# Modulation-weight loads asked for one step later: the ring of buffers keeps one load less ahead

## Chip, cores and metric

The kernel runs on one core of a Trainium2 chip. The metric is the device time of one execution in microseconds (us). Five engines work side by side, each on its own list of instructions in program order: TensorE (PE in the profile, its weight loads PEld), VectorE (DVE), ScalarE (ACT), GpSimd (POOL) and SyncE (SP). In this kernel SyncE computes nothing; its list is a queue of transfers that it issues one after the other, each as soon as what that transfer has to wait for is done.

## What is computed

One step of a two-layer transformer that serves 256 prompt tokens and 1024 latent tokens, width 1024, all in float32. Each layer has a token mixer and a SwiGLU channel mixer. What bears on the change is the modulation: both sub-layers of a layer are scaled, shifted and gated by vectors that come from a conditioning vector, one for latent tokens and one for the prompt.

```
mod_p = silu(c_ctx) @ w_mod[l] + b_mod[l]      # (6*1024,), w_mod[l] is (1024, 6144)
mod_s = silu(c)     @ w_mod[l] + b_mod[l]
sh1, sc1, g1, sh2, sc2, g2 = split(mod, 6)     # for each of the two
x = x + g1 * mixer(rms_norm(x) * (1 + sc1) + sh1)
x = x + g2 * swiglu(rms_norm(x) * (1 + sc2) + sh2)
```

The matrices w_mod hold 2 x 1024 x 6144 numbers, some 50 MB, and are read once.

## The kernel before

The stages follow each other: input projection of layer 0, its attention, its output projection (`out_proj`), its channel mixer (`ffn`), then the same four for layer 1. Weights of the dense products come through `Weights`: a 512 KB piece is loaded into `wraw` or `wrawx` (L251), and split into a high and a low part `whl` by ScalarE (L280) and VectorE (L282) four pieces ahead of use. When a piece has been split, its buffer is given back and the next 512 KB load goes into SP's queue.

The modulation vectors of later sub-layers are made in the background of these stages by the class `Mod`, on VectorE. A job is 512 columns of `w_mod` for one layer; it has 8 tiles of 128 x 512 (256 KB). One call of `step` takes one tile: two VectorE instructions (L386 or L388) multiply it by the two conditioning columns and add it to two accumulators `nacc`. After the eighth tile two calls do nothing, then two calls sum the accumulators over the partitions (four transposes on TensorE each, L400, and a VectorE reduction, L401), and a last call adds the bias (`mod_done`, L324). So a job takes 13 calls, 8 of which use a tile.

The tiles sit in a ring of `bufs` buffers. The constructor asks for the first `bufs` loads; then each step that has used a tile asks for a further one (L318 through `load`). Program order alone decides where that transfer stands in SP's queue. There are four rings:

- input projection of layer 0: 4 jobs, `bufs` 4, tile `wmod`; up to two steps for each dense product
- output projection of layer 0: 2 jobs, `bufs` 3, tile `wmod`; two steps after a dense product
- channel mixer of layer 0: 12 jobs, 96 tiles, `bufs` 2, the two halves of one tile `st`
- channel mixer of layer 1: 2 jobs, 16 tiles, `bufs` 2, the same

In `ffn` a hidden slice i (22 of them) goes through `front`, `prompt_gate` and `back`. From i = 2 on, each slice calls `mstep`, which is one `step`, six times, here in the order of the program, with the transfers that are put into SP's queue between the calls:

```
front(i):  product Q11, mstep, product Q21 -> c (L925)
prompt_gate(i):                W.done       -> weight load (L251)
back(i):   product T2 (L1004), mstep
           product T1,         W.done       -> weight load, mstep
           product T3 (L1017), mstep
           product Q22 (L1027) -> spill of H (L900), W.done -> weight load, mstep
           prompt product -> spill (L945), product T4 -> spill (L900),
                               W.done       -> weight load, mstep
```

The last `mstep` of a slice and the first of the next have only the product Q11 between them, which ScalarE reads out; so VectorE does their four instructions in a row. The weight load ahead of that pair waits for the L282 that VectorE does just before the pair.

After the slices come six rounds `down(q)` that multiply the stored hidden values `hd` by the down weights (matmuls L1063 to L1065, each result added into `x` by VectorE at L1067). Round q loads its slabs `A<-hd` by `load_h` (L905, three transfers of 1 to 2 MB), asked for two rounds ahead, and `load_x` brings back `x<-xr` (L911, 24 transfers). In the rounds one `mstep` follows each output row block. PSUM results of the dense stages use a ring of 8 banks (`psd`).

Of the kernel before, what the change touches and what calls it, by code (L numbers as in the profile page):

```python
# [123 lines left out]
def hybrid_step(ctx: ExitStack, tc: tile.TileContext, I: dict, O: list):  # L124
# [67 lines left out]
    class Background:  # L192
# [12 lines left out]
        def step(self, n=1, now=1 << 30):  # L205
            for _ in range(n):
                if not self.q or self.q[0][1] > now or self.q.pop(0)[2]():
                    return
# [112 lines left out]
    def mod_done(l, j, v):  # L321

        o = modv[:, l, 4 * j:4 * j + 4, :]
        dve.tensor_tensor(o, v, bmod[:, l, 4 * j:4 * j + 4, None].to_broadcast([128, 4, 2]), op=OP.add)  # L324
        six, half = j // 2, j % 2
        if six in (1, 4):
            k = six // 4
            g = norms[:, 2 * l + k, 4 * half:4 * half + 4, None].to_broadcast([128, 4, 2])
            dve.scalar_tensor_tensor(moda[:, l, k, 4 * half:4 * half + 4, :], o, 1.0, g, op0=OP.add, op1=OP.mult)
# [27 lines left out]
    class Mod:  # L357
# [14 lines left out]
        def step(self):  # L372
            if self.pending:
                f = self.pending.pop(0)
                if f:
                    f()
                return True
            if self.pos >= len(self.tiles):
                return False
            l, j, k = self.tiles[self.pos]  # L380
            t = self.loaded.pop(self.pos)[:, 0]
            if k == 0:
                self.acc = [(self.sums or npool).tile([128, 512], F32, name="nacc", bufs=2) for _ in range(2)]
            for c, a in enumerate(self.acc):
                if k == 0:
                    dve.tensor_scalar(a, t, cond_raw[:, k, c:c + 1], 0.0, op0=OP.mult, op1=OP.add)  # L386
                else:
                    dve.scalar_tensor_tensor(a, t, cond_raw[:, k, c:c + 1], a, op0=OP.mult, op1=OP.add)  # L388
            self.pos += 1
            self.load(self.pos + self.bufs)  # L390
            if k == 7:
                acc, v = self.acc, npool.tile([128, 32], F32, name="mv", bufs=2)[:, 0:8].rearrange("p (b x) -> p b x", x=2)
                self.pending = [None, None, lambda: self.sum(acc[0], v, 0), lambda: self.sum(acc[1], v, 1),
                                lambda: mod_done(l, j, v)]
            return True
# [1326 lines left out]
```

## Time and profile before

| | us |
|---|---|
| median of 3 runs | 3082.54 |
| lowest, highest | 3079.99, 3093.14 |
| the profiled execution, its own time | 3094.04 |
| its span, first to last instruction | 3092.3 |
| mean granted clock of TensorE in it | 0.975 |

The profiled execution is one run; 1.7 us of its time lie outside the span. It is 11.5 us above the median of the three unprofiled runs. Times within the trace are counted from the start of the span.

### The profile page before, as it was taken

What the parts mean: (1) busy time and instruction counts of PE and PEld (TensorE: products, weight loads), DVE (VectorE), ACT (ScalarE), POOL (GpSimd) and SP (SyncE); (2) the same over time, 40 slices, a digit from 0 to 9 for tenths busy, and PEclk for the clock granted to TensorE, in tenths of its full rate; (3) what the DMA queues carried; (4) which work ended last, traced back from release to release, by engine and by line L of the source; (5) the groups of instructions that cost most, each with busy time, mean ns of one, the idle gap of its engine ahead of it and who ended that gap; (6) DMA issues with size and microseconds to landing.
All of it is one profiled execution on the core that took longest, in us unless ns stands there. A gap on an engine that the chain in (4) does not pass through costs nothing.

```text
span 3092.3 us, 46174 instructions
## 1 busy us (share of the span) xinstructions
PE 2937.8 (95%) x18074; PEld 2489.7 (81%) x18074; DVE 1875.6 (61%) x3035; ACT 1089.3 (35%) x2084; POOL 822.8 (27%) x692
## 2 busy tenths in 40 slices
PE   6999999988999999899999999999789999999998
PEld 4878777867888887788878777878678888888887
DVE  5654665577777776544455688862767555554334
ACT  4233773343333332000332577761433333330002
POOL 0241542232333332000222344431323333320002
PEclk9999999989999999999999999999899999999999
DMA  6467644213434436543133410123033223255421
GB/s 248 146 194 228 154 128 154 89 49 129 136 127 130 133 126 237 203 172 138 68 122 141 154 59 31 36 83 99 24 130 116 92 93 101 102 180 204 177 102 69
DMA packets 184330, 394.55 MB, mean 128 GB/s; under 512 B 32176, under 2 KB 69424, under 8 KB 177840
## 3 DMA queue, kind: packets, MB, share of 16 engines
q1 hardware_dynamic: 180656, 385.34, 36.7%
q0 software_dynamic: 3456, 6.26, 0.8%
q8 instruction: 143, 2.34, 0.3%
q14 instruction: 75, 0.61, 0.1%
HBM read 274.32 MB, written 118.23 MB: 127 GB/s over the span
## 4 chain that ended last, share of the span: by engine, by line
PE 68%; DVE 11%; ACT 5%; issue 3%; POOL 3%; DMA 2%; SPq 0%; DVEq 0%; ACTq 0%; POOLq 0%
PE psd L1063 6%; PE psd L1065 6%; PE psd L1064 6%; PE psd L307 6%; PE psd L309 6%; PE psd L308 6%; PE psd L884 6%; PE psd L885 6%; PE psd L886 6%; PE ps_t L684 5%; PE ps_o L700 5%; PE ps_s L632 4%; DVE nacc L388 2%; ACT whl L280 2%; DVE whl L282 2%
## 5 line engine op out<-in xcount | busy, mean ns | idle before, releaser
L308 PE MATMUL psd<-A,whl 128*128 128x256 f32 (+1 forms) x1760 | 585.9, 333 | 16.0 <-DVE A L490 15.0
L307 PE MATMUL psd<-A,whl 128*128 128x256 f32 (+1 forms) x1760 | 588.9, 335 | 7.3 <-ACT A L454 2.7
L309 PE MATMUL psd<-A,whl 128*128 128x256 f32 (+1 forms) x1760 | 583.1, 331 | 2.0 <-DVE whl L282 2.0
L280 ACT ACTIVATE whl<-wraw 128x1024 fp32r<-128x1024 f32 x178 | 187.1, 1055 | 649.7 <-PE psd L1065 461.2
L1063 PE MATMUL psd<-A,whl 128*128 128x512 f32 (+1 forms) x1056 | 378.1, 358 | 16.3 <-DVE x L1067 10.3
L308 PEld LDWEIGHTS psd<-A,whl 128*128 128x128 f32 x1760 | 341.6, 194 | 52.5 <-DVE A L490 17.5
L1064 PE MATMUL psd<-A,whl 128*128 128x512 f32 (+1 forms) x1056 | 376.1, 356 | 0.0
L1065 PE MATMUL psd<-A,whl 128*128 128x512 f32 (+1 forms) x1056 | 376.0, 356 | 0.0
L307 PEld LDWEIGHTS psd<-A,whl 128*128 128x128 f32 x1760 | 342.2, 194 | 41.3 <-ACT A L454 3.2
L309 PEld LDWEIGHTS psd<-A,whl 128*128 128x128 f32 x1760 | 346.0, 197 | 31.7 <-DVE whl L282 3.3
L1067 DVE SCALAR_TENSOR_TENSOR x<-psd,modv,x 128x512 f32<-128x512 f32 (+1 forms) x288 | 186.9, 660 | 283.1 <-PE psd L1065 278.8
L282 DVE TENSOR_TENSOR whl<-wraw,whl 128x1024 fp32r<-128x1024 f32 x174 | 238.7, 1374 | 145.4 <-ACT whl L280 143.3
L884 PE MATMUL psd<-A,whl 128*128 128x512 f32 x704 | 277.4, 394 | 0.0
L885 PE MATMUL psd<-A,whl 128*128 128x512 f32 x704 | 275.4, 391 | 0.0
L886 PE MATMUL psd<-A,whl 128*128 128x512 f32 x704 | 275.4, 391 | 0.0
L674 POOL TENSOR_SCALAR sP<-sP,sm 128x896 f32<-128x896 f32 (+2 forms) x206 | 179.4, 875 | 245.8 <-DVE sm L667 120.0
L1063 PEld LDWEIGHTS psd<-A,whl 128*128 128x128 f32 x1056 | 201.1, 190 | 45.5 <-DVE x L1067 11.1
L1065 PEld LDWEIGHTS psd<-A,whl 128*128 128x128 f32 x1056 | 202.1, 191 | 28.0
L1064 PEld LDWEIGHTS psd<-A,whl 128*128 128x128 f32 x1056 | 201.1, 190 | 27.6
L684 PE MATMUL ps_t<-ident,sP 128*128 128x128 f32 x1408 | 206.6, 285 | 7.3 <-POOL sP L674 2.6
L426 POOL TENSOR_TENSOR nacc<-nacc,ec 128x512 f32<-128x512 f32 (+1 forms) x32 | 34.7, 1084 | 623.2 <-ACT ec L425 621.8
L684 PEld LDWEIGHTS ps_t<-ident,sP 128*128 128x128 f32 x1408 | 152.8, 143 | 57.3 <-issue 24.5
(224 smaller groups left out, 5246.6 us busy)
## 6 DMA issues: line engine op xcount, KB each, us to landing
hd<-x SPq DMA_DIRECT2D x84, 512.0 KB, 3.1
A<-hd SPq DMA_DIRECT2D x20, 2048.0 KB, 12.3
wraw<-in_w_gu_dram SPq DMA_DIRECT2D x60, 512.0 KB, 3.6
st<-in_w_mod_dram SPq DMA_DIRECT2D x112, 256.0 KB, 2.8
wraw<-in_w_down_dram SPq DMA_DIRECT2D x44, 512.0 KB, 3.7
wrawx<-in_w_gu_dram SPq DMA_DIRECT2D x28, 512.0 KB, 3.7
A<-hd SPq DMA_DIRECT2D x14, 1024.0 KB, 14.8
wmod<-in_w_mod_dram SPq DMA_DIRECT2D x48, 256.0 KB, 3.0
```

The costliest lines, as they stand in the source:

```text
L280: act.activation(h[:, 0], src, AF.Copy)
L282: eng.tensor_tensor(h[:, 1], src, h[:, 0].bitcast(F32), op=OP.subtract)
L307: pe.matmul(ps[:, :n], wh, A[ti].part(0, k), start=(k == 0), stop=False)
L308: pe.matmul(ps[:, :n], wh, A[ti].part(1, k), start=False, stop=False)
L309: pe.matmul(ps[:, :n], wl, A[ti].part(0, k), start=False, stop=(k == 7))
L684: pe.transpose(pt[:, 128 * (i - lo):128 * (i - lo) + 128], P[u][:, 128 * j:128 * j + 128], ident)
L884: pe.matmul(pt, wh, t(0, c), start=(c == 0), stop=False)
L885: pe.matmul(pt, wh, t(1, c), start=False, stop=False)
L886: pe.matmul(pt, wl, t(0, c), start=False, stop=(c == 3))
L1063: pe.matmul(pt[:, :n], wh, t[:, 0, k], start=(k == 0), stop=False)
L1064: pe.matmul(pt[:, :n], wh, t[:, 1, k], start=False, stop=False)
L1065: pe.matmul(pt[:, :n], wl, t[:, 0, k], start=False, stop=(k == nk - 1))
```

## The change

`step` asks for loads up to `pos + bufs - 1` in place of `pos + bufs`. The constructor still asks for `bufs` loads. So the first step asks for none, and from the second step on each step asks for the load that the step before it asked for until now: each later load stands in SP's queue where the next one stood. The buffer it goes into is the same and the step that must have used that buffer is the same; what is new is that all transfers that the program puts into SP's queue between two steps now stand ahead of it. The number of loads, their size and all arithmetic stay.

```diff
             self.pos += 1
-            self.load(self.pos + self.bufs)
+            self.load(self.pos + self.bufs - 1)
             if k == 7:
```

## Rows read from the trace of the kernel before

**Rows 1.** Windows: stretch, us, busy of PE, PEld, DVE, ACT, POOL, clock, DMA, GB/s.

```profile
711.00:1208.00 497.00, 482.71 (x2594) 418.71 (x2593) 383.85 (x463) 157.59 (x234) 169.97 (x112) 0.99 0.40 131
1208.00:1265.00 57.00, 41.36 (x177) 34.07 (x175) 33.12 (x51) 5.24 (x8) 2.75 (x2) 0.85 0.85 308
1265.00:1440.00 175.00, 175.00 (x924) 151.00 (x923) 88.77 (x128) 13.62 (x13) 0.00 (x0) 1.00 0.44 160
```

**Rows 2.** Waits of VectorE, 711 to 1208: us in total, times, longest us.

```profile
DVE whl L282 <- ACT whl L280: 49.8, 46, 1.9
...
DVE ea L1027 <- POOL ea L1018: 9.0, 7, 1.5
```

**Rows 3.** Waits of TensorE, 711 to 1208.

```profile
PE psd L400 <- DVE nacc L388: 14.3, 3, 8.1
```

**Rows 4.** Timeline of SP: start us, duration, what; two stretches of the slices.

```profile
734.68 0.52 SPq L900 DMA_DIRECT2D hd<-x  x1
736.91 0.33 SPq L251 DMA_DIRECT2D wraw<-in_w_gu_dram  x1
738.24 7.31 SPq L318 DMA_DIRECT2D st<-in_w_mod_dram  x3
...
940.48 0.33 SPq L251 DMA_DIRECT2D wrawx<-in_w_gu_dram  x1
```

**Rows 5.** Timeline of VectorE: pairs of steps, first, fifth and ninth; in brackets idle time.

```profile
736.81 2.73 DVE L388 SCALAR_TENSOR_TENSOR nacc<-st,cond_raw,nacc 128x512 f32<-128x512 f32 x4
...
940.37 3.76 DVE L388 SCALAR_TENSOR_TENSOR nacc<-st,cond_raw,nacc 128x512 f32<-128x512 f32 x4
...
1124.29 2.73 DVE L388 SCALAR_TENSOR_TENSOR nacc<-st,cond_raw,nacc 128x512 f32<-128x512 f32 x4
```

**Rows 6.** Timeline of SP, start of the third ring.

```profile
705.83 0.33 SPq L251 DMA_DIRECT2D wrawx<-in_w_gu_dram  x1
706.22 5.54 SPq L318 DMA_DIRECT2D st<-in_w_mod_dram  x3
```

**Rows 7.** Timeline of VectorE, first step of the third ring.

```profile
710.52 0.88 DVE L386 TENSOR_SCALAR nacc<-st,cond_raw 128x512 f32<-128x512 f32 x2 [4.71 <-DMA st<-in_w_mod_dram]
```

**Rows 8.** Page, part 6: DMA issues, KB each, median us to landing.

```profile
st<-in_w_mod_dram SPq DMA_DIRECT2D x112, 256.0 KB, 2.8
```

**Rows 9.** Timeline of TensorE, single rows where it waited.

```profile
554.66 0.63 PE L400 MATMUL psd<-ident,nacc 128*128 128x128 f32 x4 [3.24 <-DVE nacc L388]
...
1080.62 0.66 PE L400 MATMUL psd<-ident,nacc 128*128 128x128 f32 x4 [3.41 <-DVE nacc L388]
...
1219.60 0.55 PE L1063 MATMUL psd<-A,whl 128*128 128x256 f32 x1 [5.36 <-DMA A<-hd]
...
1253.71 0.79 PE L1063 MATMUL psd<-A,whl 128*128 128x512 f32 x1 [6.48 <-DVE x L1067]
...
2319.48 1.11 PE L400 MATMUL psd<-ident,nacc 128*128 128x128 f32 x4 [9.93 <-DVE nacc L388]
```

**Rows 10.** Timeline of SP, end of the slices and first down round.

```profile
1200.95 1.31 SPq L905 DMA_DIRECT2D A<-hd  x2
...
1229.46 0.84 SPq L318 DMA_DIRECT2D st<-in_w_mod_dram  x1
...
1231.42 2.02 SPq L905 DMA_DIRECT2D A<-hd  x3
```

**Rows 11.** Timeline of VectorE, first down round.

```profile
1222.55 1.41 DVE L388 SCALAR_TENSOR_TENSOR nacc<-st,cond_raw,nacc 128x512 f32<-128x512 f32 x2
...
1236.65 1.41 DVE L388 SCALAR_TENSOR_TENSOR nacc<-st,cond_raw,nacc 128x512 f32<-128x512 f32 x2 [7.80 <-DMA st<-in_w_mod_dram]
...
1251.85 1.41 DVE L388 SCALAR_TENSOR_TENSOR nacc<-st,cond_raw,nacc 128x512 f32<-128x512 f32 x2 [9.04 <-DMA st<-in_w_mod_dram]
1253.18 1.80 DVE L1067 SCALAR_TENSOR_TENSOR x<-psd,modv,x 128x256 f32<-128x256 f32 x3
```

**Rows 12.** Timeline of VectorE, last step of the first ring.

```profile
263.75 1.42 DVE L388 SCALAR_TENSOR_TENSOR nacc<-wmod,cond_raw,nacc 128x512 f32<-128x512 f32 x2 [3.62 <-DMA wmod<-in_w_mod_dram]
```

## Prediction

> **What bounds the kernel now.** I read the profile by stages, with the sums by window first. In most stretches TensorE is never idle, so only what makes it wait counts. Three stretches hold steps of the rings with two buffers: the slices of the first channel mixer, its first down round, and the later rounds [rows 1]. In the slices TensorE is busy 482.71 of 497 us and VectorE 383.85, which looks like room on VectorE. The waits say otherwise. VectorE's waits in this stretch come to seven groups, and none of them names TensorE; the largest are for ScalarE and GpSimd instructions that themselves had to wait for a VectorE result just before [rows 2]. So VectorE runs behind TensorE all through these 497 us, and its list, with the round trips in it, is a chain without slack. TensorE feels this chain at one place only: the transposes of a finished job wait for the accumulators, three times, 14.3 us in all [rows 3]. A microsecond that VectorE loses between two such ties is therefore not absorbed; it is handed to TensorE at the next tie.
>
> **What the change does.** It removes and adds no instruction. Load n keeps its buffer, so it still waits for step n - bufs. It only moves behind the transfers that stand between its old place in SP's queue and that of load n+1. Where no transfer stands between, nothing changes. Where some do, they wait for later VectorE work, so the load is issued when the last of them has been. Whether a step is late then depends on how soon it follows.
>
> In a slice, five of six places are harmless: the step that uses the load comes after another product result, some microseconds later. The sixth is the pair of steps in a row. The load for its second step now stands behind the two spills and the weight load that precede the pair. In the first pair, the steps start at 736.81 and their four instructions take 2.73, so the second begins at about 738.1 [rows 5]. The weight load was issued at 736.91, the spill at 734.68 [rows 4]. The moved load can go no earlier than right behind that weight load, some 0.4 us later.
>
> *How late it lands.* The nearest row of before is the start of the third ring: a spill, a 512 KB weight load at 705.83 and the modulation load at 706.22, 0.39 us behind it [rows 6]; the step that needs it starts at 710.52, 4.69 us after the weight load was issued [rows 7]. By that row the second step of the pair starts at 736.91 + 4.69 = 741.60, not 738.1: VectorE stands 3.5 us. The lower bound is a load that nothing in front delays, 2.8 us [rows 8]: 736.91 + 0.39 + 2.8 = 740.1, 2.0 us. As 512 KB are ahead of it in the same queue, I stay near the upper row: 3.3.
>
> The Trainium skill (DMA: Bandwidth & Descriptors, Anatomy of one DMA) fits a transfer issued from GpSimd as 2.0 us plus its bytes at 436 GB/s. As an estimate by that page these 256 KB would take 2.6 us and the stall would be 1.8; nine of them would be 16 us in place of the 28 that I use below, and the whole sum 22, a time of 3104. The rows show this load at 2.8 in the median and at over 4 behind a weight load, so the fit lacks what stands ahead.
>
> *How many.* Nine such pairs lie in the slices of the first channel mixer, from 736.81 to 1124.29; in two of them the first step itself takes about a microsecond longer (as in the fifth, 3.76 for the four) and uses up that much of the stall [rows 5]. 7 x 3.3 + 2.3 + 2.8 = 28.2 us on VectorE. In a tenth pair only the spills are ahead, and I count it as 0.
>
> *Where they come out.* Eight of the nine lie before 1080.62, where TensorE already waits 3.41 us for an accumulator, so it takes over the whole delay there: 24.9. The ninth lies behind it. At 1219.60 TensorE waits 5.36 us for a slab [rows 9], and that slab's load is at the end of a queue that only went on, at 1200.95, when VectorE had split a weight [rows 10]. There the remaining 3.3 come out. Sum: **+28**.
>
> **The first down round.** Here VectorE already waits for modulation loads, 7.80 and 9.04 us, while TensorE stands because its PSUM banks are full [rows 9, 11]. Each load takes the place of the next. So the step at 1222.55, which did not wait, gets the landing that now ends the wait at 1236.65, and the one that now runs at 1236.65 goes directly behind it; the one that lands at 1251.85 serves the step before the one it serves now. VectorE comes out one cycle late: a step of 1.41 and three results of 1.80 together, **+3.2**, and TensorE with it, since the banks of three results are released that much later. The bounds are 0, if TensorE regained it (it doesn't wait at all from 1265 to 1440 [rows 1], so there is nothing to regain), and 7 if the longer idling also costs clock: the granted clock in this stretch is 0.85 against 1.00 behind it [rows 1].
>
> **The later rounds.** Some loads there come behind three slab loads. How long that takes is seen at 1231.42 [rows 10]: the modulation load behind those three serves the step at 1251.85 [rows 11], 20 us later. A round has a step each 7 us, so two steps, behind the two such places with a job under way, will be up to 10 us late. I count this as nothing, and the cover is the ring of PSUM banks: 924 matmuls take 175 us [rows 1], 36 of them make a row of three results, 6.8 us, so TensorE can run eight results, 18 us, ahead. Without that cover it would be up to 20.
>
> **The second channel mixer** has two such pairs. The first stands directly ahead of the job end at 2319.48, where TensorE waits 9.93 us [rows 9]: **+3.3**. Behind the second no step is left after that job, and VectorE can catch up: 0.
>
> **The other rings.** In the output projection a load moves behind a weight load and makes one of the last steps about 0.8 us late; TensorE waits for that job's end at 554.66 [rows 9]: **+0.8**, bounds 0 and 1.5. In the input projection the next to last load moves behind the load of a K slab and lands with the last, which VectorE awaits at 263.75; one step of 1.42 us then comes later [rows 12]. Two calls without work and further products follow before the sums, which cover it: 0, bound 1.4.
>
> **Sum.** 28 + 3.2 + 3.3 + 0.8 = 35.3 us. The profiled execution took 3094.04, so its like would take 3129. Its distance to the median is not the change's, so the same sum on the median of 3082.54 gives **3118**.
>
> **Rivals.**
> - *Only the ties count.* If VectorE catches up between the ends of jobs, just the stalls right ahead of a tie come through: two in the first mixer, one in the second, with the down round and the output projection 3 x 3.3 + 3.2 + 0.8 = 14, so 3096. For it: TensorE passes most job ends without waiting (three in [rows 3]). Against it: VectorE never once waits for TensorE in the stretch [rows 2], so it has nothing to catch up with.
> - *Hidden anyway.* If the load, though later in the queue, landed before its step, or ran ahead of the weight load, the slices would not change; what is left is the down round, +3: 3086. It decides if the landing takes under 0.8 us from issue, and no row comes near [rows 8].
> - *Faster: the queue comes free.* With the load's wait gone from in front of the slab loads, slabs could come earlier, at best the whole wait of 5.36 at 1219.60 [rows 9]: 3077. Against it: what follows a moved load in the queue waits for VectorE instructions that come after the step anyway.
> - *Worse by the clock.* TensorE's new waits at the job ends bring stretches at the lower of its two clocks, as around 1208 to 1265; 0.15 of these 57 us once more [rows 1] is 8.6, so 3127.
>
> **How the numbers follow.** My forecast, VectorE's chain in full: 0.68. Only the ties: 0.14. Hidden anyway: 0.07. Faster queue: 0.02. Worse by the clock: 0.09. 0.5% of the median, about what a measurement of this kernel can tell from no change, is 15.4 us: 3067 to 3098. The forecast and the clock case lie above that; the ties case, at 3096, straddles the bound, a third of it above; the hidden and the faster queue lie within, but for a small part of the last. Slower 0.81, same 0.18, faster 0.01. The range leaves out the hidden and faster cases and reaches from the ties case, 3096, to the clock case with stalls of 3.5, 3130.
>
> **What would show it.** Right: in each of the nine pairs VectorE idles 2 to 3.5 us in the middle, released by a modulation load issued 0.4 us after a weight load; waits of L388 for `st`, which the slices do not have now, come to some 28 us; TensorE's waits at L400 grow by some 25 us; the step that was at 1222.55 waits over 10 us. Wrong: pairs without a gap (then the load is not late), or gaps that do not appear at L400 or in the span (then VectorE had slack after all).

## The result, and the profile after

| | before | after |
|---|---|---|
| median of four runs, us | 3084.85 | 3123.76 |
| lowest, highest, us | 3079.99, 3093.14 | 3120.55, 3125.97 |
| the profiled execution, us | 3094.04 | 3125.97 |
| mean granted clock of TensorE in it | 0.975 | 0.971 |

The ratio is 1.0123, with a 95% interval from 1.0098 to 1.0147: 38 us slower, between 30 and 45, in place of the 35.3 forecast; the 3123.76 lie within the range given. The profiled executions are 31.9 us apart; that of before lies above all four runs in the table (3093.14 at most), and that of after is the slowest of its four. Layer 0 ran 3.3 us faster in the trace of after, up to the first step of the third ring (707.18, against 710.52 in [rows 7]). So times of after compare with those of before when 3.33, the difference before rounding, is added; I do so below where I speak of a delay.

The windows of after, laid over the same three stretches as [rows 1]:

```profile
707.00:1234.00 527.00, 492.14 (x2612) 424.56 (x2611) 383.96 (x461) 157.42 (x233) 170.44 (x112) 0.97 0.36 124
1234.00:1296.00 62.00, 39.87 (x172) 32.91 (x171) 35.83 (x56) 6.32 (x8) 2.70 (x2) 0.78 0.75 280
1296.00:1468.00 172.00, 172.00 (x911) 148.50 (x910) 85.26 (x126) 12.74 (x12) 0.00 (x0) 1.00 0.43 163
```

VectorE's 384 us of work in the slices are the same; the stretch is 30 us longer. What fills them stands in VectorE's waits from 707 to 1236, the answer to [rows 2]:

```profile
DVE whl L282 <- ACT whl L280: 53.0, 47, 1.9
DVE nacc L388 <- DMA st<-in_w_mod_dram: 28.5, 10, 4.7
...
DVE ea L1027 <- POOL ea L1018: 9.0, 7, 1.5
```

The second row is new: ten waits, 28.5 us. TensorE is still in none of these rows. The first of the ten, as SP and then VectorE saw it:

```profile
731.36 0.52 SPq L900 DMA_DIRECT2D hd<-x  x1
733.59 0.33 SPq L251 DMA_DIRECT2D wraw<-in_w_gu_dram  x1
733.97 5.60 SPq L318 DMA_DIRECT2D st<-in_w_mod_dram  x3
```

```profile
733.48 1.40 DVE L388 SCALAR_TENSOR_TENSOR nacc<-st,cond_raw,nacc 128x512 f32<-128x512 f32 x2
737.80 1.42 DVE L388 SCALAR_TENSOR_TENSOR nacc<-st,cond_raw,nacc 128x512 f32<-128x512 f32 x2 [2.92 <-DMA st<-in_w_mod_dram]
```

What was one row of four instructions in [rows 5] is two rows with a hole of 2.92 us. The load goes out 0.38 us behind the weight load and its step starts 3.83 us after that. In the nine pairs of the slices the holes are 2.92, 3.17, 4.68, 2.96, 2.00, 3.29, 2.90, 3.06 and 3.06, 28.0 in all; the tenth pair, with only spills ahead, has 0.51.

TensorE meets this at its waits. First the sum from 707 to 1240, beside [rows 3]; then single rows, in the order of [rows 9] with new ones between them:

```profile
PE psd L400 <- DVE nacc L388: 33.8, 6, 11.0
```

```profile
553.33 0.84 PE L400 MATMUL psd<-ident,nacc 128*128 128x128 f32 x3 [4.04 <-DVE nacc L388]
...
744.26 1.12 PE L400 MATMUL psd<-ident,nacc 128*128 128x128 f32 x4 [10.95 <-DVE nacc L388]
...
1102.24 1.11 PE L400 MATMUL psd<-ident,nacc 128*128 128x128 f32 x4 [5.84 <-DVE nacc L388]
...
1246.08 0.55 PE L1063 MATMUL psd<-A,whl 128*128 128x256 f32 x1 [9.10 <-DMA A<-hd]
...
1264.76 0.79 PE L1063 MATMUL psd<-A,whl 128*128 128x512 f32 x1 [7.79 <-DVE x L1067]
...
1279.64 0.79 PE L1063 MATMUL psd<-A,whl 128*128 128x512 f32 x1 [5.24 <-DVE x L1067]
...
2350.19 1.12 PE L400 MATMUL psd<-ident,nacc 128*128 128x128 f32 x4 [12.35 <-DVE nacc L388]
```

The tie that stood at 1080.62 is now at 1102.24, which is 24.95 us later once the 3.33 are added. The slab's tie, formerly 1219.60, is 29.8 later, and its wait has grown from 5.36 to 9.10. VectorE in the first down round, for [rows 11]:

```profile
1262.90 1.41 DVE L388 SCALAR_TENSOR_TENSOR nacc<-st,cond_raw,nacc 128x512 f32<-128x512 f32 x2 [13.45 <-DMA st<-in_w_mod_dram]
...
1277.77 1.42 DVE L388 SCALAR_TENSOR_TENSOR nacc<-st,cond_raw,nacc 128x512 f32<-128x512 f32 x2 [8.71 <-DMA st<-in_w_mod_dram]
...
1280.82 1.41 DVE L388 SCALAR_TENSOR_TENSOR nacc<-st,cond_raw,nacc 128x512 f32<-128x512 f32 x2
```

The step formerly at 1222.55 is the one at 1262.90. The one at 1277.77 is the step before the one that waited at 1251.85. Two steps of the later rounds, and the first pair of the second mixer:

```profile
1370.63 1.42 DVE L388 SCALAR_TENSOR_TENSOR nacc<-st,cond_raw,nacc 128x512 f32<-128x512 f32 x2 [11.00 <-DMA st<-in_w_mod_dram]
...
1424.35 1.41 DVE L388 SCALAR_TENSOR_TENSOR nacc<-st,cond_raw,nacc 128x512 f32<-128x512 f32 x2 [8.95 <-DMA st<-in_w_mod_dram]
...
2343.73 1.41 DVE L388 SCALAR_TENSOR_TENSOR nacc<-st,cond_raw,nacc 128x512 f32<-128x512 f32 x2 [3.14 <-DMA st<-in_w_mod_dram]
```

### The profile page after: what moved, and what is told of

Its sections match the earlier page's. It is cut to its first block, busy times and chain, and to the rows that moved or that the text cites. A ratio compares the mean times of both kernels' runs of the same rounds, so it can differ in the third digit from the quotient of the medians.

```text
span 3124.1 us, 46129 instructions
## 1 busy us (share of the span) xinstructions
PE 2938.6 (94%) x18074; PEld 2488.1 (80%) x18074; DVE 1877.3 (60%) x3035; ACT 1089.9 (35%) x2084; POOL 824.8 (26%) x692
## 4 chain that ended last, share of the span: by engine, by line
PE 70%; DVE 11%; ACT 6%; DMA 5%; issue 4%; POOL 3%; SPq 1%; DVEq 0%; ACTq 0%; POOLq 0%
PE psd L307 7%; PE psd L308 7%; PE psd L309 7%; PE psd L1063 6%; PE psd L1065 6%; PE psd L1064 6%; PE ps_t L684 5%; PE psd L886 5%; PE psd L885 5%; PE psd L884 5%; PE ps_o L700 5%; PE ps_s L632 4%; DVE nacc L388 2%; ACT whl L280 2%; DMA st<-in_w_mod_dram 2%
## 5 line engine op out<-in xcount | busy, mean ns | idle before, releaser
L280 ACT ACTIVATE whl<-wraw 128x1024 fp32r<-128x1024 f32 x178 | 187.1, 1055 | 655.4 <-PE psd L1065 479.0
L282 DVE TENSOR_TENSOR whl<-wraw,whl 128x1024 fp32r<-128x1024 f32 x174 | 238.6, 1373 | 145.6 <-ACT whl L280 145.2
L388 DVE SCALAR_TENSOR_TENSOR nacc<-st,cond_raw,nacc 128x512 f32<-128x512 f32 x196 | 153.4, 823 | 77.0 <-DMA st<-in_w_mod_dram 77.0
## 6 DMA issues: line engine op xcount, KB each, us to landing
A<-hd SPq DMA_DIRECT2D x20, 2048.0 KB, 12.5
```

Of the source, the lines that this page charges most:

```text
L280: act.activation(h[:, 0], src, AF.Copy)
L282: eng.tensor_tensor(h[:, 1], src, h[:, 0].bitcast(F32), op=OP.subtract)
```

## The experiments

The theory is that of the prediction: a load that falls behind a weight load makes the second step of a pair late, and VectorE, a chain without slack, passes that on to TensorE in full. Against it stand two others: that only what is late right ahead of a tie counts, and that a ring with one load less costs wherever it stands, not through the pairs. All ratios are to the kernel before in the same group of runs (its medians there were 3087.81 to 3089.29). A gain or loss in us is worked out from the ratio unless the text says that it is between medians.

### Which part carries the cost: three kernels

**First two rings alone.** The later load only where a ring has more than two buffers.

```diff
-            self.load(self.pos + self.bufs)
+            self.load(self.pos + self.bufs - (self.bufs > 2))
```

> Only the rings with 4 and 3 buffers (input and output projection of layer 0) ask one step later; the two rings with 2 buffers ask as before. Queue theory (the cost arises only where a load has moved behind transfers that wait for VectorE and its step follows at once, which is the pair of steps in the channel mixer's slices, and where it has moved behind slab loads in the first down round): +0.8 us, at most +2, all of it at the transposes near 554 us. Depth theory (one load less in flight uncovers a part of every load's latency): these are 44 of the 160 tiles, so about a quarter of the 39 us, +11. Waits of L388 and L386 for wmod: 9 us before; queue theory 9 to 12, depth theory 20 or more.

3088.10 against 3089.29, ratio 0.9997 (0.9989 to 1.0005): nothing that shows. In the trace the last tie of the output projection waits 3.70 in place of 3.24. In the five traces below whose first two rings are those of before (pair alone, later first tie, half steps before, and the two with moved steps) the same tie waits 2.83 to 5.18, so neither the 3.70 nor the 4.04 of after can be told from scatter. This kernel's mixers are those of before, so its trace is a second one of them: from the first step of the third ring to the first step of the job begun in the last slice it takes 499.4 us (704.61 to 1204.03), before 498.9 (710.52 to 1209.43), after 529.1 (707.18 to 1236.31). The 30.2 are far above the 0.5 by which the two traces of the same mixers differ.

**The pair alone.** Before, with the later load only in the last `mstep` of a slice.

```diff
-        def step(self):
+        def step(self, less=0):
...
-            self.load(self.pos + self.bufs)
+            self.load(self.pos + self.bufs - less)
...
-        def mstep():
+        def mstep(less=0):
...
-                md.step()
+                md.step(less)
...
-            mstep()
+            mstep(1)
```

> The kernel before, with one place of six changed: the step behind the Q22 product asks for one load less, so that the load for the second step of each pair is asked for by the first step of the pair, behind the spills and the weight load. All other loads stand where they stood. Queue theory: nine stalls of about 3 us in the slices of the first mixer, one tied and one free in the second, so +28 to +33, and nothing in the first down round (VectorE waits there 7.8 and 9.0 us as before). Ties only (VectorE catches up between job ends): +10. Depth theory: one place of six, +6.

3114.87, ratio 1.0087 (1.0071 to 1.0102), +27 us (25.6 between the medians), a little short of the 28 to 33 expected. Eight pairs have a hole (3.09, 3.17, 4.82, 2.95, 1.38, 3.22, 3.06, 2.88, together 24.6), and the stretch of the slices, from the first step of the third ring at 705.21 to the step at 1229.81, grows by 25.7. The one pair left, the sixth in order of time, is told apart by itself, in VectorE's timeline:

```profile
1002.45 1.91 DVE L386 TENSOR_SCALAR nacc<-st,cond_raw 128x512 f32<-128x512 f32 x2
1004.28 1.40 DVE L388 SCALAR_TENSOR_TENSOR nacc<-st,cond_raw,nacc 128x512 f32<-128x512 f32 x2
```

Here the call of the slice before used no tile and put off no load. The load for 1004.28 was issued at 981.28, and there is no hole. In the kernel after, this pair has one of 3.29.

**The pair undone.** After, with the old place only in that `mstep`.

```diff
-        def step(self):
+        def step(self, less=1):
...
-        def mstep():
+        def mstep(less=1):
...
-                md.step()
+                md.step(less)
...
-            mstep()
+            mstep(0)
```

> The changed kernel, with that one place of six as it was before: the step behind the Q22 product asks for two loads ahead. All other loads one step later. Queue theory: the pairs' gaps are gone; what is left is the first down round (+2 to +3) and the output projection (+0.8): +2 to +5 against before, no wait of L388 for st within the slices. Depth theory: five places of six remain, +32.

3094.80, ratio 1.0028 (1.0018 to 1.0038): +8.6 us (5.5 between the medians), more than the 2 to 5 expected and far from the 32 that depth as such would cost. VectorE's waits in the slices and in the first down round:

```profile
DVE nacc L388 <- DMA st<-in_w_mod_dram: 2.9, 1, 2.9
```

```profile
DVE nacc L388 <- DMA st<-in_w_mod_dram: 23.0, 3, 13.4
```

One pair is left, the one that the kernel above did not stall. The stretch of the slices grows by 5.3 us, 2.4 more than this hole; what fills those 2.4 is not traced. The down round adds 2.9 (the first step ahead of it is 3.1 us later than in the trace of before, the first one behind it 6.0). So both are small and stand in the trace, and 26.9 + 8.6 is 35.5, near the whole change (between the medians 25.6 + 5.5, 31.1).

### What makes the load late

**Load ahead of the weight load.** After, with the pair's second load asked for right before the `W.done` ahead of the pair, so that the spills still stand in front of it but the weight load does not.

```diff
+            if md is not None and now[0] > 1:
+                md.load(md.pos + 2)
             W.done(ui)
```

> The changed kernel, with the load for the second step of each pair asked for between the two spills and the weight load, instead of behind all three. Queue theory with the 512 KB ahead as the larger part of the lateness: the load goes out about 1.7 us earlier and has no weight load in front; the gap in each pair falls from 3.1 to between 0 and 0.9 us, the slices cost 0 to 8, and with the first down round the time is +3 to +11 against before. If the spills ahead were enough to make it late: gaps of 2 us and more, +20 or more.

3105.86 against 3088.18, ratio 1.0049 (1.0037 to 1.0062): +15 us, between 11 and 19 (17.7 between the medians), more than the 3 to 11 expected; somewhat over half of the loss is gone. SP's timeline and VectorE's at the first pair:

```profile
728.37 0.52 SPq L900 DMA_DIRECT2D hd<-x  x1
728.93 0.61 SPq L318 DMA_DIRECT2D st<-in_w_mod_dram  x1
730.60 0.33 SPq L251 DMA_DIRECT2D wraw<-in_w_gu_dram  x1
```

```profile
732.85 1.41 DVE L388 SCALAR_TENSOR_TENSOR nacc<-st,cond_raw,nacc 128x512 f32<-128x512 f32 x2 [0.94 <-DMA st<-in_w_mod_dram]
```

The load is issued 1.67 us ahead of the weight load and the hole shrinks from 2.92 to 0.94. It isn't gone: from 728.93 to the landing at 732.75 the 256 KB take 3.82 us, behind a spill of 512 KB issued 0.56 us before, where the page of before has 2.8 in the median [rows 8]. Over the nine pairs 9.2 us are left. So two thirds of the holes came from the weight load; the spills would have made the load late by themselves.

The Trainium skill (DMA: Bandwidth & Descriptors, Queues, rings and completion order) says that each DMA engine takes the descriptors of one ring in the order in which they were put there. The 3.82 us behind a spill agree with that; in what order the packets of the two moved, no row here shows.

In the trace the loss from the first step of the third ring to the first step of the job begun behind the first down round is 14.0 us (6.34 early against the trace of before, then 7.65 late, and nearly level from there), close to the 15 of the ratio. The 3.7 up to the difference of the medians are not placed; the profiled execution, 3101.84, lies 4.0 below the median of its own runs.

### Does VectorE have slack

**A later first tie.** Before, with three calls without work ahead of the sums of the first job of the 96-tile ring.

```diff
+                late = [None] * 3 if len(self.tiles) == 96 and self.pos == 8 else []
-                self.pending = [None, None,
+                self.pending = late + [None, None,
```

> The kernel before, with the sums of the first job of the first channel mixer put three calls (half a slice) later, where VectorE has had time to finish the accumulators; all later steps come three calls later as well. In the kernel before TensorE waits 8.06 us at these sums. Chain theory (VectorE is behind TensorE for the whole stretch, and a job end only hands its delay over): the 8 us at the first sums go, but come back at later job ends or at the first slab, where VectorE is still behind: time within 4 us of before. Ties only (VectorE catches up between job ends, so a job end met later costs nothing): -8 us or more, with TensorE's waits at L400 down from 30.7 to some 22 and no other wait grown.

3085.56 against 3087.81, ratio 0.9996 (0.9987 to 1.0005). TensorE's rows where it waited (lines from L401 on are one higher here):

```profile
805.72 1.11 PE L401 MATMUL psd<-ident,nacc 128*128 128x128 f32 x4 [6.00 <-DVE nacc L388]
...
915.74 0.66 PE L401 MATMUL psd<-ident,nacc 128*128 128x128 f32 x4 [1.05 <-DVE nacc L388]
...
1141.01 1.12 PE L401 MATMUL psd<-ident,nacc 128*128 128x128 f32 x4 [4.56 <-DVE nacc L388]
1211.91 0.55 PE L1064 MATMUL psd<-A,whl 128*128 128x256 f32 x1 [6.06 <-DMA A<-hd]
1243.37 0.79 PE L1064 MATMUL psd<-A,whl 128*128 128x512 f32 x1 [9.27 <-DVE x L1068]
```

In the trace of before the longest wait of [rows 3] stands at the first job's end:

```profile
744.58 1.12 PE L400 MATMUL psd<-ident,nacc 128*128 128x128 f32 x4 [8.06 <-DVE nacc L388]
```

It is gone, and no time is won that the interval shows: the next job's end, which did not wait before, takes 6.00, and others follow. So this tie didn't make the delay, it only showed it. VectorE waits for TensorE twice in these slices, 2.8 us together, each time some ten microseconds behind one of these ties, and nowhere else. That speaks against the theory that only the ties count.

**Half of each step, in the kernel before and in the one after.** The second instruction of a step, which adds up the prompt's modulation, is left out in the rings of two buffers for every tile of a job but its first, so the prompt's modulation vectors are not complete. It gives VectorE some 0.7 us of slack a step.

```diff
-            for c, a in enumerate(self.acc):
+            for c, a in enumerate(self.acc if k == 0 or self.bufs > 2 else self.acc[:1]):
```

> The kernel before, with the second of the two instructions of a step left out in the two rings with 2 buffers, for all tiles of a job but its first (the prompt's modulation vectors are then not what they should be). Beside the next run it tells what slack on VectorE does. VectorE has 0.67 us less for each of some 98 steps. Chain theory (VectorE's list is what holds the slices, handed over to TensorE at the job ends): TensorE's waits at L400 shrink from 30.7 us to 10 to 20, the time by -8 to -18. If TensorE alone holds the slices: within 3 us of before.

> The changed kernel with the same instructions left out. The gap in each pair grows by the 0.67 us that the first step is shorter, to about 3.8. Chain theory: VectorE now has some 4 us of room in a slice with six steps, so most of the nine gaps are made up before the next job end; this run minus the run without the second instruction on the old order is +3 to +14, against +39 between the full kernels. If every gap costs its length wherever it stands: +38 or more.

Before so cut: 3064.86, ratio 0.9920 (0.9906 to 0.9933), 23 us faster between the medians, a little beyond the 8 to 18 expected. After so cut: 3087.95, ratio 0.9995 (0.9986 to 1.0004), so the change costs 23 us between the medians of these two, not 38. First TensorE's waits and VectorE's in the cut kernel before, then the same rows in the cut kernel after, both over the slices (TensorE's over the down round too):

```profile
PE psd L400 <- DVE nacc L388: 5.1, 1, 5.1
...
DVE ea L1027 <- PE psd L886: 5.6, 3, 1.9
```

```profile
PE psd L400 <- DVE nacc L388: 15.5, 3, 8.7
...
DVE nacc L388 <- DMA st<-in_w_mod_dram: 33.3, 17, 4.3
```

With half of each step gone VectorE catches up and waits for TensorE, a row that neither the kernel before nor the one after has in the slices. And now about half of the holes is swallowed: 30.2 us in the nine pairs, longer than with whole steps, delay the sums of the last job in the slices by 12.5 (from 2.0 us earlier at the first step to 10.5 later) and the slab by 16.0. In the change itself 28.0 us of holes delay the same sums by 25.2, and the slab by 29.8. That is the condition of the theory: a hole passes in full because VectorE has no slack to lose. The 23 us are above the 3 to 14 expected, so less was made up than expected. In the cut kernel before, VectorE's wait for ScalarE's part of a weight (L282 for L280) is 68.4 us in the slices where the kernel before has 49.8, and its wait for TensorE only 5.6. In the traces 12.5 of the 23 lie in the slices, 5 in the slab wait and the down round, and 2 in the second mixer; the rest is not placed.

The Trainium skill (Perfetto Trace Analysis, Identifying the Most-Contended Engine) has one look for the engine with the highest occupancy and work on that one first; for TensorE it would have the headroom judged by the share of the peak that is reached and by the busy share of the weight loads. By either share that is TensorE in the trace of after, with matmuls at 94% of the span and weight loads at 80%, while VectorE is at 60%. That choice alone would miss what the runs show of the slices: with TensorE's dense work unchanged and VectorE's cut, the kernel is 23 us faster.

### Away from the first down round

**No steps in the first down round**, in the kernel before. The steps follow in the rounds behind it.

```diff
-            elif ti == 0:
+            elif ti == 0 and q:
```

> The kernel before, without steps in the first down round; they move into later rounds, and a few calls without a tile to the end of the fifth round. If the waits of VectorE for modulation loads (7.80 and 9.04 us) are what holds TensorE at 1238 and 1253 (3.80 and 6.48 us): these two waits of TensorE are gone, -8 to -11 us. If TensorE is held there by the slabs and the x tiles that share the transfer queue: the time stays within 2 us and TensorE's waits are named DMA A or DVE x with x<-xr.

3074.81, ratio 0.9955 (0.9940 to 0.9970): 14.5 us faster than before between the medians, where 8 to 11 were expected. TensorE's two waits for VectorE's results in that round are gone: the 6.48 of [rows 9], and this one ahead of it in the trace of before, 10.3 together.

```profile
1238.52 0.66 PE L1063 MATMUL psd<-A,whl 128*128 128x512 f32 x1 [3.80 <-DVE x L1067]
```

The windows from the first matmul on the slab to one and the same matmul further on, before and then here (the four matmuls more are transposes at L400):

```profile
1219.59:1264.93 45.34, 35.05 (x148) 29.14 (x149) 25.42 (x41) 1.44 (x3) 0.00 (x0) 0.83 0.81 304
1216.77:1245.80 29.03, 29.02 (x144) 25.03 (x145) 19.02 (x30) 1.06 (x1) 0.00 (x0) 0.94 1.04 405
```

The same work takes 16.3 us less, at a granted clock of 0.94 against 0.83: 10.3 of it are the waits, and 6.0 are a shorter busy time of TensorE, some 0.3 of them the four transposes. The waits had cost clock as well. The wait for the slab itself is 6.57 here, 1.2 longer than in [rows 9].

**And the second mixer's steps from its slice i = 8 on in place of i = 2**, with the edit above.

```diff
-            if md is not None and now[0] > 1:
+            if md is not None and now[0] > (1, 7)[l]:
```

> The kernel before without steps in the first down round, and in the second channel mixer with the first step at slice 8 instead of 2. By the waits of the kernel before: the 10.3 us of TensorE in the first down round go (as in the run without steps in that round, -14), and the 9.93 us at 2319 go if VectorE has caught up with TensorE by slice 8: -20 to -26 in all. If VectorE is still behind at slice 8, or falls behind there through the steps, the second part is 0 to -3: -14 to -17.

3060.71 against 3088.18, ratio 0.9914 (0.9901 to 0.9927): 27 us faster than the kernel before between the medians, a little beyond the 20 to 26 expected, and the best of all. TensorE's waits for accumulators over the whole span, to be read against 30.7 us in 6 waits before and 53.2 in 9 after:

```profile
PE psd L400 <- DVE nacc L388: 19.9, 5, 8.1
```

The 9.93 at the second mixer's first job end is gone; 8.07 at the first job's end in the first mixer is left, and 7.73 at the first slab.

## Why the prediction was right, and where its sizes were off

The mechanism and its places are those forecast. By term, each as the growth of a delay in the trace of after against that of before, of VectorE's to the step behind the ninth pair's slice and in the second mixer, of TensorE's in the others:

| term | predicted | measured |
|---|---|---|
| of the slices: eight pairs, at the tie formerly at 1080.62 | 24.9 | 24.95 |
| slices, to the first step behind the ninth pair's slice | 28.2, rounded to 28 | 30.2 (holes of the nine 28.0) |
| first down round | 3.2 | 1.9 |
| later rounds | 0 | 0 |
| second mixer | 3.3 | 3.15 |
| output projection | 0.8 | 0.8 (not told from scatter) |
| input projection | 0 | 0 |
| sum | 35.3 | 36.0 |

The sum is nearer than its parts: the slices came out 2.0 larger and the down round 1.3 smaller, and that these two nearly cancel is luck. Of the 30.2 in the slices, 28.0 are the nine pairs, 0.5 is the tenth, forecast at 0, and most of the rest is a weight load of the down stage that landed 6.2 us after its issue at 1225.93, where the one at 1200.58 in the trace of before took 4.5. VectorE's L282 behind it waited 1.81 us for ScalarE in place of 0.06; in six of the other traces the same wait is 0.00 to 0.65, so this belongs to that one trace and not to the change.

*The pair.* Right in sum: holes of 2.00 to 4.68 where 3.3 was taken, the fifth short by the longer first step, as forecast (2.00 against 2.3). The sixth, which also has a longer first step, has 3.29, so the 2.8 forecast for the second such pair did not come. The third is longer than the upper bound of 3.5; its load left SP at 842.61 and landed 5.5 us later. "As 512 KB are ahead of it in the same queue" names only part of the cause: the kernel with the load ahead of the weight load still has 9.2 us of holes, behind the spills alone. As the two stand one behind the other, the sum was not hurt.

*Where it comes out.* Right in sum at the tie of the eight pairs, and for the ninth at the slab. The 24.9 were to come out whole at that tie; in the trace of after TensorE takes them over in shares, with six waits at L400 where there were three, from 744.26 on. TensorE's waits at L400 grew by 19.5 us in the slices and by 2.4 in the second mixer, less than the 25 announced, though the tie at 1102.24 moved by all of 24.95. The rest is not waiting: TensorE was busy 492.14 us over the slices in place of 482.71, for nearly as many matmuls, at a granted clock of 0.97 against 0.99.

*VectorE without slack* was read from a row that was not there, its wait for TensorE. These five stand between and behind the two of [rows 2], and none names TensorE:

```profile
DVE x L768 <- ACT x L767: 27.5, 38, 0.8
DVE ea L955 <- ACT ea L954: 14.6, 19, 0.8
DVE ph L768 <- ACT ph L767: 9.2, 19, 0.5
...
DVE nacc L386 <- DMA st<-in_w_mod_dram: 4.7, 1, 4.7
DVE whl L282 <- DMA wraw<-in_w_gu_dram: 1.9, 1, 1.9
```

A row that is missing can only suggest it; the cut kernels and the later tie show it.

*The first down round* is the term that was too large. The cycle that VectorE comes out late is there, 3.05 us from 1277.77 to 1280.82, but the landing that ends the wait at 1277.77 came 29.25 us later than the one at 1251.85, 0.95 less than the 30.2 with which VectorE entered the round. In the kernel with the pair undone the round adds 2.9, in the one with the load ahead of the weight load 2.2. The granted clock of the stretch fell from 0.85 to 0.78, but what that cost lies inside the 1.9, so the rival of the clock did not come on top.

*The later rounds.* Steps wait 11.00 and 8.95 us, and TensorE's delay stays at 28.76 us, as measured without the 3.33, from the end of the first down round to the last job's sums. So they were covered, as forecast; that it is the ring of PSUM banks that does it was argued, and no run here takes it away.

*Second mixer.* On VectorE the pair came out at 3.15; TensorE's delay grew by 2.41 at that tie, from 28.30 to 30.71 without the 3.33; with this in place of the 3.15 the sum is 35.3. The second pair has a hole of 2.58, and TensorE's delay is the same 31.1 ahead of it and behind it: 0, as forecast.

*Output projection.* The wait at the tie grows by 0.8 in this trace and by 0.5 in the one of the first two rings; that the 0.8 meets the forecast is luck, since the wait scatters from 2.83 to 5.18 where these rings are as before. Over the whole time neither can be told from nothing.

The sum was set on a median of 3082.54, and came out 5.8 us below the median of after. Of these, 2.3 are the median of before, which a fourth run raised to 3084.85. The measured terms leave 2.9 of the 38.9 us between the medians unplaced, less than the interval can tell. From the first step of the third ring to the last tie that waits, the change takes 34.0 us more than the trace of before and 37.0 more than the second trace of the same mixers.

## What to carry to other kernels

How far a load runs ahead was set here not by the number of buffers alone but by its place in the queue that issues it: moved one step later, only one load of the six in a slice came too late, the one that fell behind two spills and a weight load and was wanted at once. An engine that is busy 77% of a stretch can still have no slack; look whether it ever waits for the engine that it serves, and if it does not, count each microsecond it loses as a microsecond of the kernel, as the 28.0 us of holes here came out as 29.8 at the slab. A long wait at a tie need not be where the time is lost: here the tie was moved and the wait moved along; when work was taken off the chain, it went.

## What the runs showed of the hardware

Behind some of its waits TensorE did not come back at full pace. Behind the 9.10 us at 1246.08, in the trace of after, single matmuls and then two windows (granted clock in the last column but two):

```profile
1249.20 0.62 PE L1064 MATMUL psd<-A,whl 128*128 128x512 f32 x1
1249.63 0.42 PE L1065 MATMUL psd<-A,whl 128*128 128x512 f32 x1
1249.89 0.40 PE L1063 MATMUL psd<-A,whl 128*128 128x512 f32 x1
1250.13 0.40 PE L1064 MATMUL psd<-A,whl 128*128 128x512 f32 x1
```

```profile
1246.08:1249.63 3.55, 3.55 (x11) 3.07 (x12) 3.37 (x4) 0.60 (x1) 0.00 (x0) 0.50 1.05 394
1249.89:1256.59 6.70, 6.70 (x36) 5.73 (x35) 0.00 (x0) 0.00 (x0) 0.00 (x0) 1.00 1.06 387
```

Matmuls of one shape start 0.43 us apart up to 1249.63 and 0.24 apart from 1249.89 on: the lower of the two levels of its clock, 1.2 GHz, then the higher, 2.4. So 3.55 us behind this wait went at little over half the pace, an estimate of 1.6 us on top of it. The kernel without steps in the first down round shows such a price measured: with two waits of 10.3 us together gone, TensorE was also busy for 6.0 us less over the same dense work, so that more was won than the waits that I had expected alone. It isn't so at once behind each wait: behind the 3.24 us of 554.66 in the trace of before the granted clock is still 1.00 up to 555.80, and 0.59 from 557 to 560.

The same 256 KB load took 2.8 us to land in the median of before [rows 8] and 3.6 in that of after, with the same number of loads and bytes; what stands ahead of it in SP's queue is what differs.

```profile
st<-in_w_mod_dram SPq DMA_DIRECT2D x112, 256.0 KB, 3.6
```
